# Paced mixer steps, later loads, turned units beside products and a re-ordered seam in a one-core hybrid mixer and ConvFFN kernel

## The chip, the cores and the metric

The kernel runs on one core of a Trainium2 chip. Its time is the device time of one execution in microseconds (us). Before the change it is 1338.61 us, the median of three runs (1338.36 to 1342.25).

## The reference

One step of a streaming encoder layer is computed for 1024 prompt tokens of a new stream and 32 tokens of a running one (D = 1024, FFN width 2816). Every matrix product is exact to fp32.

```python
xn = rms_norm(x, g)
parts = xn @ w_in                       # q, k, v, gates of three mixers
o = [gla(6 heads), hgrn2(5 heads), mlstm(5 heads)]   # linear recurrences with decay,
                                        # q/k of mlstm through a causal conv of width 4
h = head_rms_norm(concat(o), g_head) * silu(gate)
x = x + rms_norm(h @ w_out, g)          # sandwich norm
u, v = conv3(rms_norm(x, g) @ w_up)     # causal depthwise conv of width 3
y = x + rms_norm((gelu(u) * v) @ w_dn, g)
```

The outputs are the new x of both streams and all recurrent states.

## The kernel before

**Arithmetic.** A fp32 operand is held as two halves, h and l, in a reduced fp32 type. `mm3` (L86 to L90) makes one product of three matmuls: h by h (L88), l of one by h of the other (L89, L90). TensorE (PE) does all products and transposes (an `ident` operand); ScalarE (ACT) casts the h halves, VectorE (DVE) subtracts to get the l halves.

**Stages.** The 1024 prompt tokens are eight units of 128 tokens (0 to 7), the 32 sample tokens are unit 8. First comes `inproj`, which projects three groups g of units (0 to 2, 3 to 5, and 6, 7, 8). Before a group is projected its units are transposed on PE (tiles `xt30`, `xt31` are the two halves of unit 3), cast into `xh` by ACT and subtracted into `xl` by DVE. `pv<unit>_<block>` are products for values and gates, `pf2_0` to `pf2_13` are feature products (queries, keys, gates) of group 2, and `pv2_1_0` and the like are value products of group 2 in the other orientation, made after the features.

**Mixers beside products.** The recurrences of unit u (`mixer`) are generators that yield 12 times. `merge(main, nmain, nside)` steps a main generator and pumps mixer steps so that they advance in proportion. The mixers of group g-1 run beside the projection of group g; for group 2 there are 38 main steps and 36 mixer steps. In a mixer, `sc<u>_0`, `sc<u>_2` and `sc<u>_4` are three score products in short sub-blocks, each of which DVE masks into `P` (COPY_PREDICATED, L816) before the next may use the space; `mi` is one shared PSUM tile for transposes and state products (ACT copies it to `kt2`, L877); `og`, `oh`, `om`, `oi` are outputs, `hrs`/`hss` the head norms on POOL, `cat` the joined output (DVE L1002, POOL L1004). At its end the mixer of unit u stores `cat` to DRAM on SP's queue (`cat_d`) and the output projection loads it back as `ct`.

**Output projection.** `pipeline` runs `outproj` for units 0, 1, 2, 3, 8, 4, 5 (`RING`), each in steps: transposes `ctp<u>0`, `ctp<u>1` with their halves `ch`, `cl` (L1090, L1091), products `zp<u>0`, `zp<u>1`, norm and residual, and transposes `fxt<u>0`, `fxt<u>1` for the next stage. The mixers of units 6 and 7 run beside it. Units 6 and 7 are projected after the pipeline, in an order that is written out.

**Seam.** There the up projection of the FFN begins, a Strassen-like scheme with seven products and column operands B21, B11, T1, B22, T2, T4, T3, whose h half is cast on ACT (L1249) and whose l half is subtracted on DVE (L1250). The scheme runs block by block over the 1024 tokens in columns of 512; in the first one the operands come in two halves of 256, and the early halves of T2 and T4 lie in tiles with the names B22 and T1. So `B22l<-xg0` after 659 us is T2's l half and `T1l<-xg0` after it is T4's. `A12_1h`, `A11_1h` are weights of the next block; the two halves of a weight share a name in the trace and are told apart by engine (L93 on ACT casts, L94 on DVE subtracts). L1165 and L1166 scale unit 7's projection by its norm and add the residual.

**Order.** A scheduler lays the instructions of every engine out ahead of time; each engine then executes its row strictly in that order. Priorities, `issue_after` and the order of the generators' steps decide it.

**End.** `down_all` ends with four token tiles: L1873 adds the last partial product, L1711 squares, L1718 adds two partial sums on POOL, L206 and L207 make the reciprocal root, L1732 scales, and the result is stored.

## Time and profile before

| | us |
|---|---|
| median of three runs | 1338.61 |
| profiled execution | 1338.15 |
| its span | 1336.4 |
| PE busy | 1295.7 (97%) |
| DVE busy | 1009.2 (76%) |
| ACT busy | 700.0 (52%) |
| POOL busy | 284.6 (21%) |
| mean granted TensorE clock | 0.990 |

The profiled execution is 1338.15 us long, 1.75 us more than its span, and 0.46 us under the median. A busy PE is counted per matmul; in a row of the timeline the bracket at its end is the idle time of the engine just before it and what ended that. A windows row holds the stretch, its length, the busy time and instructions of PE, PE's weight loads, DVE, ACT and POOL, then the granted clock, the busy share of the DMA engines and GB/s.

### The profile page before, as it was taken

How to read it: one execution, taken by the hardware profiler on the slowest of the kernel's cores; microseconds unless marked ns; L12 is line 12 of the kernel's file. 1: busy time of each engine (PE TensorE's matmuls, PEld its weight loads, DVE VectorE, ACT ScalarE, POOL GpSimd, SP SyncE). 2: the span in 40 equal slices, each digit the busy share in tenths (PEclk: the TensorE clock that was granted, in tenths of full speed). 3: DMA queues.
4: the chain of work that ended last, by engine and by line, in shares of the span. 5: the costliest groups of instructions: out<-in, count | busy, mean ns of one | idle time of the engine just before them, and what ended most of it. 6: DMA issues, size and time to landing. Idle time of an engine off the chain costs nothing.

```text
span 1336.4 us, 25589 instructions
## 1 busy us (share of the span) xinstructions
PE 1295.7 (97%) x9896; PEld 1097.9 (82%) x9896; DVE 1009.2 (76%) x1761; ACT 700.0 (52%) x1298; POOL 284.6 (21%) x400
## 2 busy tenths in 40 slices
PE   6999999998999999999999999999999999999997
PEld 6999899998898987867887777778888887778885
DVE  5795659768588778785898776778888976499556
ACT  5655556554575555444764444444555454454552
POOL 4532302135022163223110010111110000020005
PEclk9999999999998999989999999999999999999999
DMA  9799878886789954534436988864665349844425
GB/s 336 246 360 367 280 258 260 275 278 214 260 263 309 330 180 163 184 111 135 143 133 216 365 223 284 213 185 135 158 162 145 88 147 350 330 146 148 139 87 126
DMA packets 134785, 291.73 MB, mean 218 GB/s; under 512 B 29016, under 2 KB 63992, under 8 KB 132536
## 3 DMA queue, kind: packets, MB, share of 16 engines
q1 hardware_dynamic: 120887, 266.51, 58.4%
q0 software_dynamic: 9264, 19.14, 7.8%
q10 hardware_dynamic: 4512, 4.46, 1.0%
q8 instruction: 77, 1.26, 0.4%
q14 instruction: 45, 0.36, 0.1%
HBM read 229.38 MB, written 85.78 MB: 236 GB/s over the span
## 4 chain that ended last, share of the span: by engine, by line
PE 63%; DVE 9%; ACT 2%; issue 1%; POOL 1%; DMA 0%; DVEq 0%; POOLq 0%; ACTq 0%
PE pux_None L88 4%; PE pux_None L90 4%; PE pux_None L89 4%; PE puw_None L89 3%; PE puw_None L90 3%; PE puw_None L88 3%; PE q L88 3%; PE q L89 3%; PE q L90 3%; PE x L88 2%; PE x L89 2%; PE x L90 2%; PE zp L88 2%; PE zp L90 2%; PE zp L89 2%; PE us L1475 2%
## 5 line engine op out<-in xcount | busy, mean ns | idle before, releaser
L1442 DVE SCALAR_TENSOR_TENSOR y<-uu,fconv_sb,y 128x1024 f32<-128x1024 f32 x88 | 112.8, 1281 | 24.7 <-ACT y L1440 23.7
L1439 POOL COPY fhalo<-uu 128x2 f32<-128x2 f32 x44 | 19.3, 439 | 380.7 <-DVE uu L1352 380.7
L1440 ACT ACTIVATE y<-uu,fconv_sb 128x1024 f32<-128x1024 f32 x44 | 54.7, 1244 | 12.8 <-DVE uu L1352 12.2
L88 PE MATMUL pv<-wt_0h,xh 128*128 128x256 f32 (+1 forms) x192 | 56.0, 292 | 2.8 <-DVE xl L319 1.6
L90 PE MATMUL zp<-woh,cl 128*128 128x512 f32 (+1 forms) x144 | 57.0, 396 | 1.5 <-DVE cl L1091 1.5
L88 PE MATMUL zp<-woh,ch 128*128 128x512 f32 (+1 forms) x144 | 56.5, 401 | 0.7 <-ACT ch L1090 0.7
L89 PE MATMUL zp<-wol,ch 128*128 128x512 f32 (+1 forms) x144 | 56.9, 395 | 0.0
L90 PE MATMUL pv<-wt_1h,xl 128*128 128x256 f32 (+1 forms) x192 | 55.1, 287 | 0.0
L90 PE MATMUL pv<-wt_0h,xl 128*128 128x256 f32 (+1 forms) x192 | 54.8, 286 | 0.0
L88 PE MATMUL pv<-wt_1h,xh 128*128 128x256 f32 (+1 forms) x192 | 54.8, 285 | 0.0
L89 PE MATMUL pv<-wt_0l,xh 128*128 128x256 f32 (+1 forms) x192 | 54.7, 285 | 0.0
L89 PE MATMUL pv<-wt_1l,xh 128*128 128x256 f32 (+1 forms) x192 | 54.5, 284 | 0.0
L206 POOL TENSOR_SCALAR hrs<-hss 128x5 f32<-128x5 f32 (+3 forms) x27 | 10.1, 375 | 174.2 <-DVE hss L1000 170.3
L1718 POOL TENSOR_TENSOR gss<-gss 128x1 f32<-128x1 f32 (+1 forms) x9 | 9.8, 1092 | 174.2 <-ACT gjk L1711 174.2
L816 DVE COPY_PREDICATED P<-masks_sb,sc 128x352 f32<-128x352 int32 (+3 forms) x53 | 37.8, 713 | 6.0 <-PE sc L729 5.4
L88 PEld LDWEIGHTS pv<-wt_0h,xh 128*128 128x128 f32 x192 | 36.2, 188 | 4.3 <-DVE xl L319 1.9
L88 PEld LDWEIGHTS pv<-wt_1h,xh 128*128 128x128 f32 x192 | 36.2, 189 | 0.7 <-issue 0.6
L1000 DVE TENSOR_REDUCE hss<-sq 128x5 f32<-128x320 f32 (+3 forms) x27 | 13.5, 502 | 30.7 <-ACT sq L999 30.6
L207 POOL TENSOR_TENSOR hrs<-hrs,mhalf 128x5 f32<-128x5 f32 (+3 forms) x27 | 36.2, 1341 | 2.2
L90 PEld LDWEIGHTS pv<-wt_0h,xl 128*128 128x128 f32 x192 | 36.4, 189 | 0.2
L89 PEld LDWEIGHTS pv<-wt_0l,xh 128*128 128x128 f32 x192 | 36.3, 189 | 0.1
L89 PEld LDWEIGHTS pv<-wt_1l,xh 128*128 128x128 f32 x192 | 36.2, 189 | 0.1
(1899 smaller groups left out, 4639.9 us busy)
## 6 DMA issues: line engine op xcount, KB each, us to landing
wus<-in_w_us SPq DMA_DIRECT2D x16, 1024.0 KB
wrP<-in_w_dn SPq DMA_DIRECT2D x27, 512.0 KB, 3.7
ht<-h_d SPq DMA_DIRECT2D x22, 512.0 KB, 7.9
wt_0r<-in_w_tok SPq DMA_DIRECT2D x21, 512.0 KB, 6.0
wt_1r<-in_w_tok SPq DMA_DIRECT2D x21, 512.0 KB, 6.1
h_d<-y SPq DMA_DIRECT2D x21, 512.0 KB, 4.4
ws_d<-in_w_dn POOLq DMA_DIRECT2D x20, 512.0 KB, 7.0
wrP<-ws_d SPq DMA_DIRECT2D x20, 512.0 KB, 3.9
```

The costliest lines, as they stand in the source:

```text
L88: pe.matmul(ps, lh[0], rh[0], start=first, stop=False, **kw)
L89: pe.matmul(ps, lh[0], rh[1], start=False, stop=False, **kw)
L90: return pe.matmul(ps, lh[1], rh[0], start=False, stop=last, **kw)
L206: pool.tensor_scalar(out, ss, 1.0 / width, eps, op0=ALU.mult, op1=ALU.add)
L207: pool.tensor_tensor(out, out, mhalf[:n, :cols], op=ALU.pow)
L816: dve.copy_predicated(dst, mk.broadcast_to([n, 11, *mk.shape[2:]]), src)
L1000: dve.tensor_reduce(ss[:n, h0:h0 + nh], sq3, axis=mybir.AxisListType.X, op=ALU.add)
L1439: behind["POOL"] = pool.tensor_copy(fhalo[:, j, :], u[:, SEQ - 2:SEQ])
L1440: act.activation(y, u, AF.Identity, scale=fconv[:, j, 2:3], bias=fconv[:, j, 3:4])
L1442: dve.scalar_tensor_tensor(y, uu[i][:, s:s + SEQ], fconv[:, j, s:s + 1], y, op0=ALU.mult, op1=ALU.add)
L1475: kept["us"] = pe.matmul(ps[DEC * q:DEC * q + DEC], smp_x[:, k, :], ring[i % 3][:, q, :], start=k == 0, stop=k == 7)
L1718: pool.tensor_tensor(ss[:n, 0:1], ss[:n, 2:3], ss[:n, 3:4], op=ALU.add)
```

## The change

1. **Turned units.** The three groups share one pair of tiles `xh_all`, `xl_all`. `inproj` receives the generator that turns the next group's units and steps it inside block 7, after unit 0's product. So units 3 and 6 are transposed between products of the group before, and the others follow one place earlier.
2. **Pace.** `merge` takes a table of (main step, mixer steps done) for group 2: one mixer step per main step in the first three, nine in the next seven, three in the seven after those, then one per step.
3. **Loads.** A mixer loads `v` one step later and `vm`, `gt` two steps later than before, all on SP's queue. The `cat_d` store goes from SP's queue to POOL's.
4. **Output projection.** Unit 6 yields like the others and is stepped inside the pipeline; unit 4's `fxt` uses another PSUM pool.
5. **Norms.** Square is taken with scale 1/32, so that two partial sums are means already and one POOL instruction adds both and eps; the separate POOL add (L1161, L1718) is gone.
6. **Seam.** T2's halves are made ahead of unit 6's last steps; unit 7's scaling (L1165) waits until T2's l half is done, unit 6's second square until T2's h half is.
7. **End.** The last add of `down_all` (L1873) gets a high priority.

```diff
-    def inproj(g, xh, xl, normed, scaled=None):
+    def inproj(g, xh, xl, normed, following, scaled=None):
...
                 vg_store(blk, u, off, n, ps)
+                if blk == 7 and not i:
+                    next(following)
                 yield
...
+    PACE = ((0, 0), (3, 3), (10, 12), (17, 15), (NIN, 3 * NMIX))
+    normed = [norm_group(g, *norm_tiles(g)) for g in range(3)] + [None]
...
-        merge(inproj(g, *xs_, norm_group(g, *xs_), scaled), NIN, n_side)
+        merge(inproj(g, *xs_, *normed[g:g + 2], scaled), NIN, n_side, PACE if g == 2 else None)
...
-            sp.dma_start(cat_d[t0:t0 + n, :], cat[:n])
+            pool.dma_start(cat_d[t0:t0 + n, :], cat[:n])
...
-            if u in RING:
+            if u != 7:
                 yield
-        if u not in RING:
+        if u == 7:
             yield
...
-        pool.tensor_tensor(ss[:n, 2:3], ss[:n, 0:1], ss[:n, 1:2], op=ALU.add)
-        rstd_of(ss[:n, 3:4], ss[:n, 2:3], n, 1, 1024)
+        rstd_of_halves(ss[:n, 3:4], ss[:n, 0:1], ss[:n, 1:2], n)
         if u == 7:
             for hf in range(2):
-                dve.scalar_tensor_tensor(pss[hf], pss[hf], ss[:, 3:4], gm[:, cs[hf]], op0=ALU.mult, op1=ALU.mult)
+                with tc.issue_after(kept["T2l"].ins):
+                    dve.scalar_tensor_tensor(pss[hf], pss[hf], ss[:, 3:4], gm[:, cs[hf]], op0=ALU.mult, op1=ALU.mult)
...
-    merge(pipeline(firsts), 26, 3 * NMIX + 2)
+    merge(pipeline(firsts, last[0]), 26, 3 * NMIX + 2)
...
     with tc.high_priority(offset=10 * AHEAD):
+        col_operands(px, q0, 0, res=X, parts="2", at_=early)
         next(last[0])
         with tc.issue_after(kept["t4"].ins):
             next(last[1])
-        col_operands(px, q0, 0, res=X, parts="t", at_=early)
+        col_operands(px, q0, 0, res=X, parts="4", at_=early)
...
-            dve.tensor_tensor(CA[:, i, 1], CA[:, i, 1], W[i], op=ALU.add)
+            with tc.high_priority(offset=AHEAD):
+                dve.tensor_tensor(CA[:, i, 1], CA[:, i, 1], W[i], op=ALU.add)
```

Three places show how the rows of the engines move. (Numbers behind the last underscore of a name only count the tiles.)

**PE, in the output projection, between the mixer of unit 7's second and third score product.** Before:

```order
L729 MATMUL sm7_8113<-ident_123,mqk7_7906 128x64
L88 MATMUL zp81_8323<-woh7_6898,ch81_8034 32x512
L89 MATMUL zp81_8323<-wol7_6906,ch81_8034 32x512
L90 MATMUL zp81_8323<-woh7_6898,cl81_8035 32x512
L1086 MATMUL ctp41_8386<-ident_123,ct4_7889 128x128 x4
L1195 MATMUL fxt30_8395<-ident_123,z3_7845 128x128 x4
L729 MATMUL sc7_4_8179<-Qz1_153,Ld1_151 64x2x32
```

The same place after the change, without the 20 matmuls in the middle of `zp40`:

```order
L738 MATMUL sm7_8105<-ident_123,mqk7_7899 128x64
L1207 MATMUL fxt30_8387<-ident_123,z3_7838 128x128 x4
L1207 MATMUL fxt31_8393<-ident_123,z3_7838 128x128 x4
L88 MATMUL zp40_8429<-woh0_6887,ch40_8246 128x512
L89 MATMUL zp40_8429<-wol0_6895,ch40_8246 128x512
...
L89 MATMUL zp40_8429<-wol7_6902,ch41_8383 128x512
L90 MATMUL zp40_8429<-woh7_6894,cl41_8384 128x512
L1097 MATMUL ctp50_8458<-ident_123,ct5_8239 128x128 x4
L738 MATMUL sc7_4_8171<-Qz1_153,Ld1_151 64x2x32
```

All 24 matmuls of `zp40`, and with them `fxt31` and `ctp50`, now stand ahead of `sc7_4`; `zp81` and `ctp41` have moved ahead of `sc7_2`.

**PE, in the features of group 2, where the transposes of unit 4's key wait for their PSUM tile.** Before, the second pair stands inside `pf2_12`:

```order
L88 MATMUL pf2_12_5572<-xh2_4320,wf2_12h_5568 128x288
L89 MATMUL pf2_12_5572<-xl2_4321,wf2_12h_5568 128x288
L90 MATMUL pf2_12_5572<-xh2_4320,wf2_12l_5569 128x288
L88 MATMUL pf2_12_5572<-xh2_4320,wf2_12h_5568 128x288
L89 MATMUL pf2_12_5572<-xl2_4321,wf2_12h_5568 128x288
L729 MATMUL mi_159<-ident_123,kh4_5305 128x128 x2
```

After the change it stands right behind `rows2` (the gates' rows, turned to columns) and ahead of `pf2_11`:

```order
L90 MATMUL pf2_10_5380<-xh_all_162,wf2_10l_5377 128x288
L629 MATMUL rows2_5433<-r_dc_2_5010,cf_sb_112 128x5 x3
L631 MATMUL rows2_5433<-ident_123,r_st_2_4999 128x128 x2
L631 MATMUL rows2_5433<-ident_123,r_st_2_4999 32x128
L738 MATMUL mi_159<-ident_123,kh4_5161 128x128 x2
L88 MATMUL pf2_11_5451<-xh_all_162,wf2_11h_5447 128x288
```

The pair has moved ahead of 29 products; `sc4_0` and the first pair have moved ahead too, in front of `pf2_10`.

**DVE, in the seam, around the l half of the weight A12 of the second block.** Before:

```order
L1352 TENSOR_TENSOR uu0_8877<-c6_00_8991,puw0_0_8913 128x256
L1250 TENSOR_TENSOR B22l_8834<-xg1_8868,B22h_8833 128x4x128
L1425 TENSOR_TENSOR uu0_8877<-uu0_8877,puv0_0_8940 128x256
L1199 TENSOR_TENSOR xg1_8868<-fxt71_9034,gcols_sb_108 128x4x128
L94 TENSOR_TENSOR A12_1h_9106<-wu1r_8972,A12_1h_9106 128x512
```

After the change:

```order
L1271 TENSOR_TENSOR xg2_8947<-xg1_8857,xg2_8947 128x4x128
L1363 TENSOR_TENSOR uu1_8867<-c5_00_8963,pux0_0_8899 128x256
L1363 TENSOR_TENSOR uu1_8867<-c7_00_9072,puz0_0_8901 128x256
L1275 TENSOR_TENSOR xg1_8857<-xg1_8857 128x1024
L1262 TENSOR_TENSOR B22l_8823<-xg1_8857,B22h_8822 128x4x128
L94 TENSOR_TENSOR A12_1h_9093<-wu1r_8959,A12_1h_9093 128x512
```

The two additions into `uu1` and the large subtraction (L1263 before, L1275 now) stood behind A12's l half and now stand ahead of it; the two additions into `uu0` have moved further up.

## The prediction

> **What bounds the kernel now.** I first cut the span into its stages and compared busy time with length (the windows view: start and end, length, then busy time and instructions of PE, its weight loads, DVE, ACT, POOL, then the granted clock).

> ```profile
> 130.00:350.00 220.00, 214.40 (x2582) 199.62 (x2581) 156.40 (x362) 124.81 (x256) 67.59 (x94) 0.99 0.79 259
> 350.00:690.00 340.00, 324.74 (x3586) 278.94 (x3586) 270.13 (x587) 190.90 (x409) 90.18 (x143) 0.97 0.60 195
> 690.00:1326.00 636.00, 636.00 (x2916) 503.03 (x2915) 484.81 (x666) 313.84 (x511) 73.08 (x100) 1.00 0.63 196
> 1326.00:1336.40 10.40, 0.76 (x4) 0.29 (x2) 6.04 (x9) 0.72 (x2) 3.21 (x7) 0.68 0.40 151
> ```

> From 690 to 1326 us PE is busy all the time at full clock. The change removes no matmul, so nothing is to be had there. PE stands idle for 220 - 214.40 = 5.6 us in the first stretch and 15.3 us in the second, and in both the clock is below 1. The last 10 us hold no products; a chain over DVE, ACT and POOL ends the kernel there. What the change can give lies in these idle times, the half-speed stretches and the last chain. Next I looked for the single waits in PE's timeline (the bracket is the wait ahead of the row and what ended it):

> ```profile
> 141.72 0.39 PE L88 MATMUL pv<-wt_0h,xh 128*128 128x256 f32 x1 [0.83 <-DVE vth L425]
> ...
> 322.44 0.81 PE L729 MATMUL oi<-C,mqz 128*64 128x65 f32 x20 [0.90 <-DVE cat L1002]
> ...
> 325.43 0.66 PE L315 MATMUL xt<-ident,x 128*128 128x128 f32 x4 [0.72 <-ACT vth L98]
> ...
> 329.45 0.45 PE L88 MATMUL pv<-wt_0h,xh 128*128 128x282 f32 x1 [1.64 <-DVE xl L319]
> ...
> 384.28 0.80 PE L729 MATMUL oi<-C,mqz 128*64 128x65 f32 x20 [0.84 <-DVE cat L1002]
> ...
> 398.82 0.44 PE L729 MATMUL mi<-ident,kh 128*128 128x128 f32 x2 [0.38 <-ACT kt L877]
> ...
> 401.66 0.67 PE L729 MATMUL sc<-Qz,k 64*64 64x64 f32 x32 [0.68 <-DVE P L816]
> ...
> 413.18 1.14 PE L729 MATMUL sc<-Qz,Ld 64*64 64x64 f32 x64 [2.15 <-DVE e L543]
> ...
> 588.87 1.80 PE L729 MATMUL sc<-Qz,Ld 64*64 64x64 f32 x64 [2.44 <-DVE P L816]
> ...
> 626.93 1.26 PE L1086 MATMUL ctp<-ident,ct 128*128 128x128 f32 x8 [0.42 <-DVE z L1199]
> ...
> 628.93 0.50 PE L88 MATMUL zp<-woh,ch 128*128 128x512 f32 x1 [0.75 <-ACT ch L1090]
> ...
> 631.12 0.50 PE L90 MATMUL zp<-woh,cl 128*128 128x512 f32 x1 [1.46 <-DVE cl L1091]
> ...
> 660.80 0.39 PE L89 MATMUL pux<-B22l,S_0h 128*128 128x256 f32 x1 [0.67 <-DVE B22l L1250]
> ```

> Then the granted clock behind the three longest of them, and around those of 0.42, 0.75 and 1.46 us:

> ```profile
> 329.60:333.10 3.50, 3.50 (x16) 3.49 (x17) 3.50 (x14) 1.76 (x5) 1.96 (x2) 0.51 0.67 267
> ...
> 415.00:422.00 7.00, 7.00 (x63) 6.39 (x63) 5.91 (x13) 1.43 (x4) 0.00 (x0) 0.51 0.73 204
> ...
> 589.00:596.00 7.00, 7.00 (x121) 6.33 (x120) 6.56 (x12) 1.15 (x2) 0.54 (x2) 0.51 0.24 80
> ...
> 625.00:650.00 25.00, 22.38 (x110) 17.96 (x109) 18.73 (x24) 16.66 (x36) 3.41 (x8) 1.00 0.44 147
> ```

> Behind the waits of 1.64, 2.15 and 2.44 us PE ran at half speed for 3.5, 7 and 7 us, which loses 0.49 of each: 1.7, 3.4 and 3.4 us. The group with 1.46 us (631.12) left the clock full, as the last row shows. I therefore price a wait of 1.6 us or more with such a stretch behind it, where PE was also short of work around it.

> [...]

> **The change part by part**, against the profiled time of 1338.15 us (0.46 under the median).

> *Third score product of unit 7.* Before, PE has little to do between the second and the third score product:

> ```profile
> 584.47 0.27 PE L729 MATMUL sm<-ident,mqk 64*128 64x64 f32 x1
> ...
> 587.80 0.92 DVE L816 COPY_PREDICATED P<-masks_sb,sc 128x352 f32<-128x352 int32 x1
> ...
> 595.96 0.48 PE L88 MATMUL zp<-woh,ch 128*128 128x512 f32 x1
> ...
> 601.30 0.39 PE L90 MATMUL zp<-woh,cl 128*128 128x512 f32 x1
> ```

> The mask copy ends at 588.72, 4.0 us behind `sm`. In the new order `zp40` stands between (24 matmuls from 595.96 to about 601.5, so 5.5 us at full clock), and two transposes beside it (1.2 us). Cover 6.7 us against 4.0 needed: the wait of 2.44 goes, and the 3.4 us of half speed with it. **-5.8** (bounds -2.4, if the clock falls there anyway, and -5.8).

> *Unit 6's projection.* `ctp60` moves ahead of `zp51`, `ctp61` between the `fxt4` halves; casts and subtractions then lie beside 24 products. The waits of 0.42, 0.75 and 1.46 go: **-2.6** (bounds -1.5 and -2.6).

> *Seam.* T2's l half needs only its ACT cast, and DVE makes it before unit 7's scaling instead of after: the wait of 0.67 goes. But the third product of the pair now follows in the same PSUM tile and must wait for ACT's copy (first row), +0.4, and A12's l half falls behind three operations that stood after it:

> ```profile
> 658.97 0.35 ACT L1347 COPY c<-pux 128x256 f32<-128x256 f32 x1
> ...
> 670.83 0.68 DVE L94 TENSOR_TENSOR A_1h<-wu1r,A_1h 128x512 fp32r<-128x512 f32 x1
> ...
> 671.98 0.40 PE L90 MATMUL puy_None<-B21h,A_1h 128*128 128x512 f32 x1
> ...
> 672.63 1.22 DVE L1263 TENSOR_TENSOR xg<-xg 128x1024 f32<-128x1024 f32 x1
> ...
> 674.37 0.41 DVE L1352 TENSOR_TENSOR uu<-c,pux 128x256 f32<-128x256 f32 x1
> ```

> 1.22 + 2 x 0.41 = 2.0 later than 671.5, of which I take off 0.5 for waits of DVE in that stretch. PE used A12's half 0.5 us after it was there, so it waits about 1.4, less two small waits near it. In sum **+1.0** (bounds -0.9, if the three fit in DVE's own waits, and +2.4).

> *End.* The last add stood behind a scaling that has nothing to do with it, and one POOL add lay in the chain:

> ```profile
> 1328.05 0.75 DVE L1732 SCALAR_TENSOR_TENSOR fr<-ca,gss,fr 128x512 f32<-128x512 f32 x1
> ...
> 1328.71 0.68 DVE L1873 TENSOR_TENSOR ca<-ca,q 128x512 f32<-128x512 f32 x1
> ...
> 1330.28 0.70 POOL L1718 TENSOR_TENSOR gss<-gss 128x1 f32<-128x1 f32 x1 [2.35 <-ACT gjk L1711]
> ...
> 1331.07 0.19 POOL L206 TENSOR_SCALAR gss<-gss 128x1 f32<-128x1 f32 x1
> ```

> Moved ahead of the second scaling of that tile and of its own queue's delay, the add gains 0.8. Of POOL's first two steps one goes; the first after a rest takes 0.70, the second 0.19 and 0.08 to start, so I take 0.3. **-1.1** (bounds -0.3 and -1.7). The same add goes from the tiles of the output projection too; PE waits for none of those, so nothing.

> *Turned units 3, 4 and 5.* `xt30`, `mi` and `xt31` now stand ahead of `pv1_7`, whose 24 matmuls covered ACT's work. The second pair of `mi` has to wait for ACT to empty the first:

> ```profile
> 143.00 0.39 ACT L98 ACTIVATE vth<-pv 128x256 f32<-128x256 f32 x1
> ...
> 145.40 0.73 ACT L877 COPY kt<-mi 64x256 f32<-64x256 f32 x2
> ...
> 150.53 0.58 ACT L318 CAST xh<-xt 128x512 fp32r<-128x512 f32 x1
> ```

> Behind 143.0 ACT runs 0.39, 0.58 and 0.73, so to 144.7; PE starts `xt30` at 141.7 as it now starts `pv`, needs about 0.7 for it (the rate of the `xt` row above) and 0.1 for one `mi`, and waits 2.2. A second wait of 0.4 for `xl`, less 0.3 that is saved, makes 2.3 less small overlaps: +2.0. It is longer than 1.64, in a place with few other products, so I add that stretch's 1.7. **+3.7** (bounds +0.5 and +3.7).

> *Turned units 6, 7 and 8.* The products of block 7 stand between `xt60` and the `xl` that was waited for; of the old 0.90, 0.72 and 1.64 us about as much stays in smaller pieces, since DVE is behind there: oi 1.9 instead of 0.9, the others 0.5, 0.5 and 1.1. That is +0.7, with the half-speed stretch of 1.7 gone: **-1.0** (bounds -3.4 and +1.7).

> *Pace and loads in group 2.* The steps of unit 3 and 4 come earlier against the products, so the 0.84 and 0.68 go. The third score product of unit 4 stands ahead of `pv2_1_0` now, but behind `pf2_12` and `pf2_13` undivided; the mask copy is the end of a DVE row that has no gaps there, and I find it 2.4 us earlier and PE's wait 1.8 instead of 2.15, with the same half-speed stretch. The new price is at the second pair of `mi`:

> ```profile
> 394.36 0.38 PE L88 MATMUL pf<-xh,wf_11h 128*128 128x288 f32 x1
> ...
> 397.62 0.29 PE L88 MATMUL pf<-xh,wf_12h 128*128 128x288 f32 x1
> ...
> 398.02 0.74 ACT L877 COPY kt<-mi 64x256 f32<-64x256 f32 x2
> ```

> Before, PE came there at 398.44. Without `pf2_11` (3.26), five of `pf2_12` (0.6) and the 0.84 it comes at 393.7. ACT's copy stands behind its casts and gates as before and I find it ending at 396.5, so PE waits 2.8 instead of 0.38. Sum -0.84 - 0.68 - 0.35 + 2.4 = **+0.5** (bounds -7, if both waits and the clock's loss go, and +4, if the copy stays at 398.8 and the clock falls once more).

> The later loads and the store on POOL's queue: the loads' first users come a step later still, and PE waited for a `cat_d` load once. POOL's small copies of the convolution's edge now stand behind the store; their reader has several us to spare. Nothing, but see the second rival.

> Sum: -5.8 - 2.6 + 1.0 - 1.1 + 3.7 - 1.0 + 0.5 = -5.3, so 1332.8 against the profile and **1333.3** against the median.

> **The rivals.**

> *The clock falls at every new wait* (0.24). Three waits of about 2 us are new or stay (322, 394, seam). If each brings 1.7 more, the sum is -0.2: 1338.4. For it: three of three waits above 1.6 us did so. Against: 660 to 680 us is full of large products.

> *POOL's queue becomes a wait* (0.11, the slower side). The store of `cat` must wait for its last scaling; the convolution's edge copies, the gates `vg` and the next norms of that queue stand behind it. Where it is issued later than those copies' readers need them, ACT's row stops with them, and DVE and PE next. It decides once the store comes over about 4 us later than its neighbours. At 2.44 us, the longest wait seen, for six units: +14.6, so 1348.

> *The mixers run so far ahead that group 2 has no wait at all* (0.17). Then group 2 gives -7 and units 3 to 5 only +0.5: -16, so 1322.6. For it: DVE and ACT have idle time before 390 us, which the earlier steps use.

> *The clock has nothing to do with the waits* (0.06). Then -2.4, -2.6, +1.0, -1.1, +2.0, +0.7, +0.5: -1.9, so 1336.7. Against it stand the three rows of the clock. [...]

> *The forecast* has 0.42.

> **How the numbers follow.** A measurement of this kernel can tell about 0.3%, that is 4 us, so faster ends at 1334.6. Of the forecast's own 0.42 some 0.31 lies below that (its bounds reach further down than up), 0.09 within and 0.02 above; the third rival is faster; 0.04 of the first and 0.01 of the last come out faster. The first rival's rest is the same but for 0.03, the last's rest is the same, the second is slower. Faster 0.53, same 0.31, slower 0.16. The range reaches to the third rival below and above the first: 1323.5 to 1342.

> **What would show it.** Right: no wait ahead of `sc7_4` and full clock there; no wait at `ch`, `cl` of unit 6; the last add 0.8 us sooner behind the last matmul; new waits at `mi` behind `xt30` and `rows2`, and at A12. Wrong: half speed still in 580 to 600 us, or no new wait at `mi`. PE idle between 690 us and the end would overturn the whole.

## The result and the profile after

The changed kernel takes **1327.89 us** (median of four, 1325.50 to 1330.28), the kernel before beside it 1339.73 us. The ratio is 0.991, with a 95% interval from 0.9884 to 0.9935: 0.9% faster, within the range given. The gain is 11.8 us, more than twice the 5.3 us of the forecast's sum. The profiled execution has 1326.90 us with a span of 1325.1 us, 11.3 us less than before.

The windows view of the changed kernel, with the columns of the prediction's first fence (the third row ends with the last product):

```profile
130.00:350.00 220.00, 214.54 (x2598) 200.20 (x2597) 154.14 (x362) 126.99 (x262) 68.69 (x99) 0.99 0.78 259
350.00:690.00 340.00, 330.16 (x3618) 283.96 (x3617) 280.99 (x603) 195.83 (x415) 94.59 (x139) 0.98 0.63 208
690.00:1316.00 626.00, 626.00 (x2871) 494.58 (x2869) 475.92 (x653) 306.28 (x501) 68.60 (x92) 1.00 0.64 191
1316.00:1325.00 9.00, 0.05 (x1) 0.00 (x0) 5.23 (x9) 0.72 (x2) 3.37 (x4) 0.71 0.47 175
```

From 690 us on nothing changed but the start: PE is busy throughout, as before. In the second stretch PE's idle time fell from 15.3 to 9.8 us, and its clock rose from 0.97 to 0.98. PE's timeline shows the waits that are left (what was L729 is L738 now, L88 to L90 are the same):

```profile
144.21 0.44 PE L738 MATMUL mi<-ident,kh 128*128 128x128 f32 x2 [2.07 <-ACT kt L888]
...
323.91 0.30 PE L738 MATMUL oi<-C,mqz 128*64 128x65 f32 x3 [1.07 <-DVE cat L1013]
...
394.34 0.44 PE L738 MATMUL mi<-ident,kh 128*128 128x128 f32 x2 [3.10 <-ACT kt L888]
395.09 0.58 PE L88 MATMUL pf<-xh_all,wf_11h 128*128 128x288 f32 x1 [0.31 <-DVE q L567]
...
588.88 1.14 PE L738 MATMUL sc<-Qz,Ld 64*64 64x64 f32 x64 [0.19 <-DVE P L827]
...
658.47 0.50 PE L88 MATMUL puy_None<-B21h,A_1h 128*128 128x512 f32 x1 [1.55 <-ACT A_1h L93]
659.51 0.50 PE L88 MATMUL pux_None<-B11h,A_1h 128*128 128x512 f32 x1 [0.31 <-ACT A_1h L93]
660.59 0.52 PE L90 MATMUL puy_None<-B21h,A_1h 128*128 128x512 f32 x1 [0.35 <-DVE A_1h L94]
```

The three new waits stand where the prediction had them: at `mi` behind `xt30` (2.07), at `mi` behind `rows2` (3.10), and at A12 (1.55). The wait of 2.44 us ahead of unit 7's third score product is 0.19 us now; those at `ctp`, `ch` and `cl` of unit 6 are gone. The clock around these places:

```profile
145.60:149.00 3.40, 3.40 (x24) 2.95 (x23) 3.08 (x9) 1.89 (x5) 2.04 (x4) 0.51 0.56 154
394.80:398.20 3.40, 3.11 (x13) 3.14 (x14) 3.34 (x9) 3.34 (x11) 0.58 (x2) 0.51 0.94 295
589.00:596.00 7.00, 7.00 (x135) 5.80 (x137) 4.76 (x9) 0.32 (x1) 0.00 (x0) 1.00 0.35 98
661.00:664.40 3.40, 3.40 (x10) 2.63 (x9) 3.40 (x6) 0.00 (x0) 0.00 (x0) 0.51 0.00 0
```

Half speed follows the new waits, and 589 to 596 us runs at full clock. At the end:

```profile
1315.66 0.39 PE L90 MATMUL q<-P3w,P3h 128*128 128x512 f32 x1
...
1317.21 0.68 DVE L1884 TENSOR_TENSOR ca<-ca,q 128x512 f32<-128x512 f32 x1
...
1318.81 1.18 POOL L211 TENSOR_SCALAR gss<-gss 128x1 f32<-128x1 f32 x1 [1.09 <-ACT gjk L1722]
```

The last add starts 1.16 us behind the last product's end (1316.05); before, it was 1.95 us (1328.71 less 1326.76). POOL's one instruction takes 1.18 us here, more than the two of before together (0.70, 0.08 to start, 0.19), so its part of the gain did not come.

To see where the time went, I cut the profiled executions at the first product of a few tiles: from `pv0_0` to `pf1_0` (units 3 to 5 are turned in it), to `pf2_2` (units 6 to 8), to `zp20` (group 2 and the start of the output projection), to `zp50` (the mixer of unit 7), to `zp70` (unit 6's projection), to `puy4` (the seam). Behind it lie 587.9 us in both.

| us | to pf1_0 | to pf2_2 | to zp20 | to zp50 | to zp70 | to puy4 | end |
|---|---|---|---|---|---|---|---|
| before | 186.4 | 171.7 | 161.8 | 83.1 | 28.5 | 95.9 | 9.6 |
| after | 188.7 | 167.2 | 160.1 | 77.9 | 25.0 | 97.8 | 9.1 |
| difference | +2.3 | -4.5 | -1.7 | -5.2 | -3.5 | +1.9 | -0.5 |
| predicted | +3.7 | -1.0 | +0.5 | -5.8 | -2.6 | +1.0 | -1.1 |

Over the stretches up to `puy4`, PE's idle time fell by 5.8 us (21.44 to 15.69) and the time at half speed from 20.5 to 17.1 us, which is worth 1.7. The other 3.2 of 10.7 us are busy time. It is the same 7205 matmuls, in fewer pieces (PE goes over to another output tile 358 times instead of 388); that this is the reason is not shown.

### The profile page after: what moved, and what is told of

Read it like the earlier page. It is cut to its first block, busy times and chain, and to the rows that moved or that the text cites. A ratio compares the mean times of both kernels' runs of the same rounds, so it can differ in the third digit from the quotient of the medians.

```text
span 1325.1 us, 25585 instructions
## 1 busy us (share of the span) xinstructions
PE 1290.7 (97%) x9896; PEld 1095.0 (83%) x9896; DVE 1008.1 (76%) x1761; ACT 700.0 (53%) x1298; POOL 286.1 (22%) x390
## 3 DMA queue, kind: packets, MB, share of 16 engines
q8 instruction: 77, 1.26, 0.4%
## 4 chain that ended last, share of the span: by engine, by line
PE 73%; DVE 14%; DMA 4%; ACT 4%; issue 3%; POOL 2%; SPq 0%; DVEq 0%; POOLq 0%; ACTq 0%
PE pux_None L88 4%; PE pux_None L90 4%; PE pux_None L89 4%; PE puw_None L90 3%; PE puw_None L88 3%; PE puw_None L89 3%; PE q L88 3%; PE q L90 3%; PE q L89 3%; PE pv L88 3%; PE pv L89 2%; PE pv L90 2%; PE x L88 2%; PE x L89 2%; PE x L90 2%
## 5 line engine op out<-in xcount | busy, mean ns | idle before, releaser
L88 PE MATMUL pv<-wt_0h,xh_all 128*128 128x256 f32 (+1 forms) x192 | 56.1, 292 | 0.9 <-DVE xl_all L326 0.7
L89 PE MATMUL zp<-wol,ch 128*128 128x512 f32 (+1 forms) x144 | 57.0, 396 | 0.0
L88 PE MATMUL zp<-woh,ch 128*128 128x512 f32 (+1 forms) x144 | 57.0, 405 | 0.0
L90 PE MATMUL zp<-woh,cl 128*128 128x512 f32 (+1 forms) x144 | 56.6, 394 | 0.0
L90 PE MATMUL pv<-wt_0h,xl_all 128*128 128x256 f32 (+1 forms) x192 | 54.7, 285 | 0.0
L89 PE MATMUL pv<-wt_0l,xh_all 128*128 128x256 f32 (+1 forms) x192 | 54.6, 284 | 0.0
L88 PE MATMUL pv<-wt_1h,xh_all 128*128 128x256 f32 (+1 forms) x192 | 54.3, 283 | 0.0
L89 PE MATMUL pv<-wt_1l,xh_all 128*128 128x256 f32 (+1 forms) x192 | 54.3, 283 | 0.0
L90 PE MATMUL pv<-wt_1h,xl_all 128*128 128x256 f32 (+1 forms) x192 | 54.3, 283 | 0.0
L206 POOL TENSOR_SCALAR hrs<-hss 128x5 f32<-128x5 f32 (+3 forms) x27 | 10.7, 396 | 171.1 <-DVE hss L1011 166.5
L88 PEld LDWEIGHTS pv<-wt_0h,xh_all 128*128 128x128 f32 x192 | 36.4, 190 | 2.2 <-DVE xl_all L326 1.1
L89 PEld LDWEIGHTS pv<-wt_0l,xh_all 128*128 128x128 f32 x192 | 36.4, 190 | 0.1
L90 PEld LDWEIGHTS pv<-wt_0h,xl_all 128*128 128x128 f32 x192 | 36.4, 189 | 0.1
L88 PEld LDWEIGHTS pv<-wt_1h,xh_all 128*128 128x128 f32 x192 | 36.0, 187 | 0.3 <-issue 0.2
L89 PEld LDWEIGHTS pv<-wt_1l,xh_all 128*128 128x128 f32 x192 | 35.9, 187 | 0.1
```

The source lines that it names most:

```text
L88: pe.matmul(ps, lh[0], rh[0], start=first, stop=False, **kw)
L89: pe.matmul(ps, lh[0], rh[1], start=False, stop=False, **kw)
L90: return pe.matmul(ps, lh[1], rh[0], start=False, stop=last, **kw)
L206: pool.tensor_scalar(out, ss, 1.0 / width, eps, op0=ALU.mult, op1=ALU.add)
```

## The experiments

What stood to be tested: do the terms belong to the edits to which I put them down, and does the length of a wait decide the clock? All experiments but one start from the changed kernel. Times are medians; a profiled execution lies up to 4 us beside its median.

**Turning of units.** Only unit 6 turned beside products, and no unit at all:

```diff
-                if blk == 7 and not i:
+                if blk == 7 and not i and g == 1:
                     next(following)
```

> Only unit 6 is turned beside the products of the group before; unit 3 is turned where it was before the change. Numbers against the changed kernel's profiled 1326.90 us. Theory (the turned units cost 2.2 us at units 3 to 5, by a wait of 2.07 us at the second pair of mi and the half-speed stretch behind it, and bring 4.5 us at units 6 to 8): that wait and the half speed at 145 to 149 us go, 1324.7. Rival 1 (both placings belong together, since an earlier unit 3 lets all mixers behind it start earlier): units 6 to 8 and group 2 lose as much as units 3 to 5 win, 1326.9 or above. Rival 2 (the half-speed stretch does not belong to the wait): 1324.8 to 1325.3, with a half-speed stretch still near 145 to 200 us.

```diff
-                if blk == 7 and not i:
-                    next(following)
```

> No unit is turned beside products; all else as changed. Numbers against the changed kernel's profiled 1326.90 us. Theory: 2.2 us come back at units 3 to 5 and 4.5 us are lost at units 6 to 8, with the waits of 0.90, 0.72 and 1.64 us at oi, xt and pv there as before and a half-speed stretch of 3.4 us behind the last: 1329.2. Rival (the prediction's own terms, 3.7 us cost and 1.0 us gain): 1324.2. Rival 2 (the gain at units 6 to 8 came from the paced steps and the later loads and not from the turned unit): units 6 to 8 stay short, 1324.7.

Without any turning the kernel takes 1328.78 us (ratio to before 0.9917, 0.9891 to 0.9942), 0.9 more than the changed kernel, which the intervals can't tell apart. Its stretch to `pf1_0` is 187.7 us and that to `pf2_2` 173.4, against 188.7 and 167.2 with both turned, so the signs are right: the placing costs in the first and brings more in the second. 1.7 of the 173.4 come from half speed at 355.5 to 358.8 us, and 1.7 of the 187.7 from half speed at 174.5 to 177.9 us, though no long wait stands ahead of the first: from 352.0 to 355.4 us PE was busy for 3.40 of 3.40 us, almost only with small products (matmuls of 64 or fewer columns, or on 16 rows); the last section comes back to that. The profiled execution is 3.8 us above its median, so its trace overstates the difference; the theory's 1329.2 fits the median.

With unit 6 alone it takes **1336.33 us** (0.9973, 0.9958 to 0.9988), 8.4 us more. Only rival 1 allows for that, and not for its reason. The wait at `mi` in units 3 to 5 is gone (1.0 us less in that stretch), and the stretch to `pf2_2` takes 2.0 us more; but the stretch from `zp20` to `zp50`, almost 400 us behind the edit (unit 3 is turned at 141 us), takes 85.1 us instead of 77.9. PE's timeline there:

```profile
550.16 0.92 PE L738 MATMUL og<-v,P 64*64 64x64 f32 x24 [1.21 <-DVE P L827]
...
571.11 0.44 PE L738 MATMUL mi<-ident,kh 128*128 128x128 f32 x2 [0.90 <-ACT kt L888]
...
573.18 0.41 PE L88 MATMUL zp<-woh,ch 128*32 128x512 f32 x1 [1.63 <-DVE z L1211]
```

None of these waits is in the changed kernel. The scheduler (called the planner from here on) has laid PE's row out differently: all three score products of unit 7 stand ahead of `ctp41` and `zp40`. I call this the third order; the first is that of before, the second that of the changed kernel (both are in the rows of PE shown with the change). Nothing in the program's text of that stage differs.

**The pace.** The table left out, then the loads and the store too:

```diff
-        merge(inproj(g, *xs_, *normed[g:g + 2], scaled), NIN, n_side, PACE if g == 2 else None)
+        merge(inproj(g, *xs_, *normed[g:g + 2], scaled), NIN, n_side, None)
```

> The pace table is left out; the mixers of group 1 advance evenly beside group 2 again, all else as changed. Numbers against the changed kernel's profiled 1326.90 us. Theory (the pace is worth about 3.3 us: it replaces waits of 0.84 and 0.68 us and the wait of 2.15 us at the third score product of unit 4, with 6.8 us of half speed, by one of 3.10 us at mi with 3.4 us): 1330.2, with a wait near 2.2 us at sc4_4 and a half-speed stretch of 6.8 us behind it, and no long wait at mi. Rival 1 (the prediction's term: the pace costs 0.5 us): 1326.4. Rival 2 (the later loads and the turned units brought it, not the table): 1326.9 with the wait at sc4_4 gone all the same.

It takes **1339.64 us** (ratio to before 1.0002, 0.9986 to 1.0017): without the table the whole gain of 11.8 us is gone, where the theory gave the table 3.3. PE's timeline in group 2:

```profile
411.46 0.35 PE L738 MATMUL sc<-Qz,Ld 64*64 64x64 f32 x9 [4.04 <-DVE e L552]
...
454.15 0.48 PE L738 MATMUL mi<-ident,mqk 128*128 128x128 f32 x1 [2.46 <-ACT kt L888]
```

The first is the old wait at unit 4's third score product, 4.04 instead of 2.15 us: the mask copy, one operation ahead of the one that the row names, ends at 411.3 us in DVE's full row. That is 1.7 us sooner than in the kernel before, while PE comes there 3.6 us sooner (407.4 instead of 411.0): 14 products of `pv`, which lay in between, are done by then. Counted from the first product of `pf2_2` DVE's copy is no sooner at all (43.4 us behind it, 43.5 before); with the pace it ends 41.0 us behind it. So an earlier PE is worth nothing here until DVE's work is put earlier too. The stretch to `zp20` takes 170.8 us instead of 160.1 (in an execution 2.9 us above its median), and that to `zp50` 83.7: the third order once more.

```diff
+        v = mx.tile([128, 704], F32, tag="v", name=f"v{u}", bufs=1)
+        sp.dma_start(v[:n], v_d[t0:t0 + n, :704])
+        vmt = vm[0]
+        sp.dma_start(vmt[:n, :, :64], v_d[t0:t0 + n, 704:].rearrange("t (h d) -> t h d", d=64))
+        gt = mx.tile([128, 1024], F32, tag="gt", name=f"gt{u}", bufs=1)
+        sp.dma_start(gt[:n], g_d[t0:t0 + n, :])
...
-        v = mx.tile([128, 704], F32, tag="v", name=f"v{u}", bufs=1)
-        sp.dma_start(v[:n], v_d[t0:t0 + n, :704])
...
-            pool.dma_start(cat_d[t0:t0 + n, :], cat[:n])
+            sp.dma_start(cat_d[t0:t0 + n, :], cat[:n])
```

> The changed kernel without the pace table and with v, vm, gt loaded where they were and the store of cat on its old queue. Numbers against the changed kernel's profiled 1326.90 us; without the table alone it was 10.0 us at the start of the output projection (9.3 behind, 0.7 of it from before group 2) and 7 to 8 us in it. Theory (with even steps the later loads and POOL's store cost, so taking them back brings group 2 to what it was before the change, about 4.5 us behind the changed kernel; the order of the output projection is the third one again, 5.8 us): 1337.2. Rival (the loads and the store do nothing): as without the table, 1339.6 or more, the wait of 4.0 us at sc4_4 and that of 2.5 us at mi as there.

It takes 1337.30 us (0.998, 0.9969 to 0.9991), as the theory had it (1337.2). The stretch to `zp20` is 164.5 us: the wait of 4.0 us stays, that of 2.46 us is gone (ahead of it ACT had stood 2.39 us for a store of `vg`). Between these two executions the later loads and the store cost 6.3 us there; the medians of twelve runs each lie only 2.3 us apart, so how much they cost with even steps stays open.

The same edit of the loads with the pace kept:

> The changed kernel with v, vm, gt loaded where they were and the store of cat on its old queue, the pace table kept. The order of the output projection stays that of the changed kernel. Numbers against the changed kernel's profiled 1326.90 us. Theory (the pace carries the gain in group 2, the loads are worth nothing beside it): within 1 us of 1326.9. Rival 1 (the prediction's second rival turned round: the store on POOL's queue costs, so taking it back gains): 1325 or less. Rival 2 (the earlier loads hold SP's queue or the buffers back, so that a mixer step waits for them): 1330 or more, with new waits on a load in DVE's or ACT's row.

It takes 1327.43 us (0.9905, 0.9888 to 0.9923): no difference from the changed kernel. Beside the pace the loads and the store together are worth nothing. So the 14.6 us of the prediction's slower rival, the store on POOL's queue, did not come; the store was not put back by itself.

**Unit 6 in the pipeline**, undone:

```diff
-            if u != 7:
+            if u in RING:
...
-    merge(pipeline(firsts, last[0]), 26, 3 * NMIX + 2)
+    merge(pipeline(firsts), 26, 3 * NMIX + 2)
```

> Unit 6's projection is not stepped inside the pipeline (the output-projection part of the change undone), all else as changed. Numbers against the changed kernel's profiled 1326.90 us. Theory: the wait of 2.44 us ahead of the third score product of unit 7, the half-speed stretch behind it (5.0 us together) and the waits at ctp60, ch and cl (3.5 us) come back: 1335.4. Rival 1 (the clock has nothing to do with the wait): 2.4 and 2.6 us come back, 1331.9, and the clock around 589 us is full. Rival 2 (the paced steps and the loads brought the gain at sc7_4 and not the new order of the output projection): only the 3.5 us come back, 1330.4.

It takes 1331.28 us (0.9935, 0.9915 to 0.9955), 3.4 more: rival 2. The stretch to `zp50` stays at 78.0 us without a wait at unit 7, and that to `zp70` takes 30.1:

```profile
621.25 1.25 PE L1097 MATMUL ctp<-ident,ct 128*128 128x128 f32 x8 [0.42 <-DVE z L1211]
623.26 0.50 PE L88 MATMUL zp<-woh,ch 128*128 128x512 f32 x1 [0.75 <-ACT ch L1101]
625.45 0.50 PE L90 MATMUL zp<-woh,cl 128*128 128x512 f32 x1 [1.45 <-DVE cl L1102]
```

These are the three waits of before, to 0.01 us. So this part brings unit 6's own term and nothing of the 5 us at unit 7.

**The norms.** Which edit had moved unit 7's score product? The one that I had priced at nothing: POOL's add in the tiles of the output projection. It alone put back:

```diff
-        rstd_of_halves(ss[:n, 3:4], ss[:n, 0:1], ss[:n, 1:2], n)
+        pool.tensor_tensor(ss[:n, 2:3], ss[:n, 0:1], ss[:n, 1:2], op=ALU.add)
+        rstd_of(ss[:n, 3:4], ss[:n, 2:3], n, 1, 1)
         if u == 7:
```

> The output projection alone has its separate POOL add of the two partial sums back (nine tiles, one small instruction each, at the place it had before); all else as changed. In the planner's order this puts the third score product of unit 7 ahead of unit 4's product again. Numbers against the changed kernel's profiled 1326.90 us. Theory (the gain at that score product comes from the order alone, and the order was turned by POOL's shorter chain): the wait of about 2.4 us and half speed near 585 us come back, 5.0 us, 1331.9. Rival 1 (the prediction: the add in these tiles is worth nothing, and unit 6 stepped inside the pipeline brought the gain): 1326.9. Rival 2 (the clock has nothing to do with the wait): 1329.3.

It takes 1332.06 us (0.9951, 0.9932 to 0.9969), 4.2 more; the theory had 1331.9. PE's row is in the first order again, and the wait is back in its old place:

```profile
585.87 0.34 PE L738 MATMUL sc<-Qz,Ld 64*64 64x64 f32 x8 [2.45 <-DVE P L827]
```

And the kernel before with this edit alone:

```diff
-            act.activation(z[:n, cs[hf]], ps[:n], AF.Square, accum_out=ss[:n, hf:hf + 1])
+            act.activation(z[:n, cs[hf]], ps[:n], AF.Square, scale=1.0 / 32, accum_out=ss[:n, hf:hf + 1])
...
-        pool.tensor_tensor(ss[:n, 2:3], ss[:n, 0:1], ss[:n, 1:2], op=ALU.add)
-        rstd_of(ss[:n, 3:4], ss[:n, 2:3], n, 1, 1024)
+        pool.tensor_scalar(ss[:n, 3:4], ss[:n, 0:1], ss[:n, 1:2], EPS, op0=ALU.add, op1=ALU.add)
+        pool.tensor_tensor(ss[:n, 3:4], ss[:n, 3:4], mhalf[:n, :1], op=ALU.pow)
```

> The kernel before, with nothing changed but the norms of the output projection (the square with scale 1/32, one POOL instruction fewer in each of nine tiles). The planner's order of the output projection becomes a third one: the three score products of unit 7 stand earlier than in either kernel, zp40 behind all of them. Numbers against the kernel before's profiled 1338.15 us; the stretch from the first product of zp20 to the first of zp50 took 83.1 us there, 77.9 us in the changed kernel, and 83.7 us in the run without the pace, which has this third order. Theory (only the order that the planner comes to counts, and edits do not add up): 83.7 us, 1338.8, with waits at og of unit 7 and at zp80, zp81 and none of 2.4 us at the third score product. Rival 1 (the norm edit by itself carries the gain of 5 us there, since putting it back cost that): 78 us, 1333.0. Rival 2 (it does nothing without the other edits): 83.1 us, 1338.2, the wait of 2.4 us in its old place.

It takes 1337.74 us (0.9992, 0.9977 to 1.0007): no change, with the waits of the third order.

```profile
555.27 0.92 PE L729 MATMUL og<-v,P 64*64 64x64 f32 x24 [1.37 <-DVE P L816]
...
576.15 0.44 PE L729 MATMUL mi<-ident,kh 128*128 128x128 f32 x2 [0.90 <-ACT kt L877]
...
578.22 0.42 PE L88 MATMUL zp<-woh,ch 128*32 128x512 f32 x1 [1.63 <-DVE z L1199]
```

The stretch takes 82.1 us (1.6 under the 83.7 expected, since here the clock stayed full behind the last wait, 1.00 from 577 to 595 us). So the same edit brings 3.7 us in one program (81.6 to 77.9) and about 1 us in another (83.1 to 82.1, the clock's luck included).

**The seam**, undone:

```diff
-                with tc.issue_after(kept["T2l"].ins):
+                if True:
...
-        with tc.issue_after(kept["T2"].ins) if u == 6 else ExitStack():
+        if True:
...
-        col_operands(px, q0, 0, res=X, parts="2", at_=early)
...
-        col_operands(px, q0, 0, res=X, parts="4", at_=early)
+        col_operands(px, q0, 0, res=X, parts="t", at_=early)
```

> The seam part is undone (T2 and T4 made together behind the last units' steps, unit 7's scaling and unit 6's second square wait for nothing more); all else as changed. Numbers against the changed kernel's profiled 1326.90 us. Theory (the seam part costs 1.9 us, by the waits of 1.55, 0.31 and 0.35 us for the halves of A12 and the half speed behind them, less the 0.67 us for T2): 1325.0, full clock at 661 to 665 us. Rival 1 (the prediction's term of 1.0): 1325.9. Rival 2 (the waits at A12 come from DVE's work as a whole and stay, T2's wait comes back as well): 1327.6.

It takes 1328.40 us (0.9915, 0.9898 to 0.9932), not to be told from the changed kernel; the theory's 1325.0 is missed, rival 2 fits. The wait at T2 is 0.72 us again, and PE waits 1.22 us for A12's l half:

```profile
652.17 0.39 PE L89 MATMUL pux<-B22l,S_0h 128*128 128x256 f32 x1 [0.72 <-DVE B22l L1262]
...
664.30 0.68 PE L90 MATMUL puy_None<-B21h,A_1h 128*128 128x512 f32 x1 [1.22 <-DVE A_1h L94]
```

The stretch to `puy4` takes 97.5 us against 97.8, both with a half-speed step (1.7). With the new seam but full clock it takes 96.4 us in five other runs; with the old seam and full clock 95.9 (before) and 96.2 (norms alone). The seam part itself costs about 0.4 us. The wait of 1.22 us is not that of the kernel before (0.24 us for A11's h half there), but it is in the run of the norms alone, too: it came with the norms.

Those copies that stand ahead of A12's cast on ACT, moved to POOL:

```diff
-                        act.copy(t[:, :, :256], e)
+                        pool.tensor_copy(t[:, :, :256], e)
```

> The changed kernel, with the four copies of the early halves of T2 and T4 into the whole tiles made by POOL, which is idle in the seam, and not by ACT, where they stand 4.2 us ahead of the cast of A12's first half. Numbers against the changed kernel's profiled 1326.90 us. Theory (the waits of 1.55, 0.31 and 0.35 us at A12 are due to those copies): 2.2 us less, and 1.7 us more where half speed followed, 1323.0 to 1324.7. Rival 1 (DVE's own row is as late there): 1326.5, a wait of similar size for A12's l half. Rival 2 (POOL's copies are slow and the whole T2 and T4 come late): 1328 or more, with a new wait at the products with T2 or T4 of the second block.

It takes 1331.67 us (0.9944, 0.9927 to 0.9961), 3.8 more. A12 no longer waits, but others do:

```profile
655.87 1.09 PE L1207 MATMUL fxt<-ident,z 128*128 128x128 f32 x8 [1.51 <-ACT z L1190]
...
657.98 0.39 PE L88 MATMUL puy<-B21h,A_0h 128*128 128x256 f32 x1 [1.02 <-ACT B21h L1261]
...
659.24 0.56 PE L89 MATMUL puy<-B21l,A_0h 128*128 128x256 f32 x1 [0.87 <-DVE B21l L1262]
```

Freed of the copies, ACT's row was laid out anew, and PE's transposes and early products with it; they now come before their operands. The time is rival 2's, the place is not.

**The two waits at `mi`.** The second pair of transposes in another PSUM tile, for units 0 and 4:

```diff
-                kps = small(2, 128)
+                kps = psm.tile([128, 2, 128], F32, tag="o", name=f"kp{u}", bufs=2) if f0 and u in (0, 4) else small(2, 128)
```

> The changed kernel, with the second pair of key transposes of units 0 and 4 in a PSUM tile of the outputs' pool instead of the shared tile mi, so that PE need not wait for ACT to empty the first pair. Numbers against the changed kernel's profiled 1326.90 us. Theory (the waits of 2.07 and 3.10 us at mi with 3.4 us of half speed behind each are pure loss): 8.5 us less, 1318.4, full clock at 145 and 395 us. Rival 1 (DVE and ACT are behind there, and the next score products wait instead): 1 to 3 us less, 1325, with new waits at sc of unit 0 or 4. Rival 2 (the clock has nothing to do with the waits): 5.2 us less, 1321.7, with two more half-speed stretches elsewhere.

It takes 1328.82 us (0.9918, 0.9906 to 0.9930): no gain. The place is rival 1's; of its 1 to 3 us nothing came.

```profile
144.63 0.56 PE L738 MATMUL sc<-Qz,k 64*64 64x64 f32 x25 [2.51 <-issue]
...
398.02 0.61 PE L88 MATMUL pf<-xh_all,wf_11h 128*128 128x288 f32 x1 [4.34 <-DVE q L567]
```

The next instruction waits instead, and longer: the score product, and `pf2_11` for its PSUM bank. In the changed kernel `pf2_11` already waited 0.31 us for the same DVE operation, right behind the wait of 3.10: that small row said beforehand that the long one had a second wait behind it.

**The clock.** Eleven waits of different length, in the down projection:

```diff
...
+                if (kind, p) in LADDER:
+                    for j in range(2):
+                        with tc.issue_after(behind["PE"].ins):
+                            behind["PE"] = pe.matmul(banks[3][:16], zero, w[0], start=False, stop=False,
+                                                     skip_group_check=True)
+                        for _ in range(0 if j else LADDER[kind, p]):
+                            pool.memset(zero.bitcast(F32), 0.0)
```

> The changed kernel with eleven waits made on purpose in the down projection, where PE was busy all the time at full clock: two small products with zeros (they add nothing to the sums), and between them 3 to 18 small POOL instructions for which the second one waits, so waits from about 0.5 to 3.5 us, each on its own. It measures what kind of wait lowers the clock. Theory 1 (the clock is set anew in steps of 3.41 us, and a step is at half speed where PE was idle for 1.6 us or more of the step before): no stretch behind waits below 1.5 us, one behind each above 3.2 us, and of those between only where most of the wait lies in one step. Theory 2 (the prediction's: the length of the wait decides, from 1.6 us up): a stretch behind every wait of 1.6 us or more. Theory 3 (only an idle step of 3.4 us does it): none, or one behind the longest alone. The whole takes about 1360 us.

It took 1373.43 us in its one execution (the last wait became 11.8 us, since POOL had other work there). Four of the waits in PE's timeline:

```profile
1186.42 0.41 PE L1711 MATMUL q<-P4w,zero 128*16 128x512 f32 x1 [2.48 <-POOL zero L1714]
...
1233.37 0.55 PE L1711 MATMUL x<-P6w,zero 128*16 128x512 f32 x1 [2.14 <-POOL zero L1714]
...
1257.83 0.61 PE L1711 MATMUL q<-P5w,zero 128*16 128x512 f32 x1 [3.15 <-POOL zero L1714]
...
1272.72 0.41 PE L1711 MATMUL q<-P5w,zero 128*16 128x512 f32 x1 [1.97 <-POOL zero L1714]
```

And the clock (the last column but two) behind each of them, in the same order:

```profile
1186.50:1189.90 3.40, 3.40 (x16) 2.79 (x17) 3.40 (x7) 2.15 (x6) 1.08 (x1) 1.00 0.14 58
...
1233.50:1236.90 3.40, 3.40 (x9) 2.62 (x9) 0.69 (x1) 0.62 (x1) 0.00 (x0) 0.50 0.00 0
1257.40:1260.80 3.40, 2.97 (x8) 2.30 (x9) 0.69 (x1) 0.62 (x1) 0.26 (x3) 0.50 0.00 0
1272.80:1276.20 3.40, 3.40 (x16) 2.79 (x17) 0.69 (x1) 0.91 (x2) 0.00 (x0) 1.00 0.00 1
```

The wait of 2.48 us left the clock full, that of 2.14 did not. That excludes a limit on the length of the wait, theory 2. Two half-speed stretches of this run start seven times 3.413 us apart (1257.364 - 1233.471 = 7 x 3.413); the last section has the starts in the kernels before and after, which lie on such a grid too. Laid on it, the wait of 2.14 us lies in one step; that of 2.48 is cut into 1.74 and 0.74. A step ran at half speed where PE had been idle for 2.14 or 2.68 us of the step before, and at full speed after 1.47, 1.63, 1.64, 1.71, 1.74 and (behind a wait of 2.06 us that nobody made, at 1100.6) 1.85 us. Theory 1 fits these steps, with its limit between 1.85 and 2.14 us instead of 1.6; theory 3 falls with the 2.14.

No run beat the changed kernel; that without the later loads is its equal.

## Why the prediction was right or wrong

**The third score product** (-5.8, measured -5.2). The wait and the half speed behind it went because `zp40` covers the mask copy: right in place, mechanism and size. What failed is a passage at the end of another part: "The same add goes from the tiles of the output projection too; PE waits for none of those, so nothing." That PE does not wait for the add does not make it worth nothing: without it the planner lays PE's row out in another order, and that is where these 5 us come from. I had read the new order and never asked which edit made it. The runs show that the edit decides (its return alone brought the wait back) and that undoing unit 6's pipeline leaves the order alone. They show, too, that the edit does so only beside some of the others: alone, without the pace, or with unit 6 alone turned, the third order comes, while with no unit turned the second one stays (78.0 us to `zp50`, 0.20 us of waiting at the third score product). Why was not traced; that the transposes of the norm's result are ready earlier in the planner's reckoning is a guess.

**Unit 6's projection** (-2.6, measured -3.5): the three waits went as said; 0.9 us of PE's busy time went with them, which I had not counted.

**Group 2** (+0.5, measured -1.7). The new wait at `mi` was forecast at 2.8 us and is 3.10. The step that failed is "PE's wait 1.8 instead of 2.15" at the third score product of unit 4, "with the same half-speed stretch": neither is left there. The mask copy did come as much earlier as I had found: counted from the first product of `pf2_2` it ends at 41.0 us instead of 43.5, 2.5 sooner for 2.4. It is PE that comes 2.3 us later than the sum has it (at 41.6 for 39.3), 0.6 behind the copy's end. Half speed follows the wait at `mi` (0.51 from 394.8 to 398.2 us) and takes 1.7 us, which my own rule asked for and the sum left out; 0.3 more of that wait and 0.31 at `pf2_11` make up the rest. So PE pays once, at `mi`, and not a second time. One of the two waits of the third rival is gone, then, but not because the mixers ran further ahead. And the term hides what the pace is worth: against even steps it brings 10.7 us in this stretch of the profiled executions (170.8 to 160.1).

**Turned units 3 to 5** (+3.7, measured +2.3): the wait is 2.07 for 2.2, with its half-speed step. The second wait, of 0.4 for `xl`, did not come. But the 2.3 is a lucky execution: eight others with unit 3 turned this way have the same wait (2.04 to 2.08 us) and take 189.3 to 190.7 us for this stretch, 2.9 to 4.3 more than before, seven of them with two half-speed steps. The forecast's 3.7 lies in the midst of these.

**Turned units 6 to 8** (-1.0, measured -4.5). I left 4.0 us of waits there, "since DVE is behind"; 1.8 us were left (1.07, 0.51, 0.23). That is the step that failed, and not in this part alone: in the run with unit 6 alone turned `oi` waits 1.95 us, as I had priced it (1.9), and it is unit 3's earlier turn that brings it to 1.07. The clock's 1.7 went as said, and 1.3 us of busy time beyond that.

**The seam** (+1.0, measured +1.9): the wait of 0.67 at T2 went and the one for ACT's copy came (0.46 for 0.4), as said. The wait at A12 is 1.55 for 1.4, but it is not the wait that I had worked out. Mine was for the l half, on DVE. In the trace PE stops for the h half, which ACT casts behind its four copies (its end is 658.41, PE goes on at 658.47), and then 0.35 us for the l half:

```profile
657.79 0.62 ACT L93 CAST A_1h<-wu1r 128x512 fp32r<-128x512 f32 x1
```

```profile
659.85 0.68 DVE L94 TENSOR_TENSOR A_1h<-wu1r,A_1h 128x512 fp32r<-128x512 f32 x1
```

So the likeness of the two numbers is luck: the sum has nothing for ACT's row there. DVE's lateness is there as well: with the h half in time PE would wait about 2.2 us for the l half (1.55, 0.31 and 0.35 together, an estimate from these rows). In itself the part costs 0.4; the rest is a half-speed step that falls there in one execution and not in another. Of the changed kernel and of the run with POOL's add back:

```profile
657.50:660.80 3.30, 1.68 (x5) 0.81 (x6) 3.30 (x7) 3.26 (x7) 0.00 (x0) 1.00 0.00 0
661.00:664.40 3.40, 3.40 (x10) 2.63 (x9) 3.40 (x6) 0.00 (x0) 0.00 (x0) 0.51 0.00 0
```

```profile
660.20:663.60 3.40, 1.85 (x14) 1.50 (x13) 3.40 (x7) 3.40 (x7) 0.00 (x0) 1.00 0.33 5
663.70:667.00 3.30, 2.63 (x10) 1.72 (x10) 3.30 (x7) 1.75 (x4) 0.00 (x0) 1.00 0.00 0
```

Both have the same waits of 1.55, 0.31 and 0.35 us (the last is 0.36 in the second), and in both the grid cuts them in two. In the first, 1.60 us lie in one step and half speed follows; in the second, 1.55 us, and it does not. In the ten profiled executions with the wait of 1.55 us, half speed came behind 1.60, 1.63, 1.86, 1.86 and 1.94 us in one step, full speed behind 1.33, 1.33, 1.55, 1.55 and 1.55.

**The end** (-1.1, measured -0.5): the add's 0.8 is right, POOL's 0.3 was not to be had.

**The clock.** "A wait of 1.6 us or more" was the wrong rule, though it gave the right answer for every wait of the changed kernel but the one in the seam. That the 1.46 us of before "left the clock full" was chance: in the run without unit 6 in the pipeline the same 1.45 us are followed by half speed (0.50 from 626.2 to 629.6 us). The rival by which the clock has nothing to do with waits falls: the waits of 2.14 and 3.15 us made in the down projection were followed by 0.50, where the changed kernel has 1.00 from 690 to 1316 us.

In sum most of the waits that I named came and went as forecast. The two terms that were off the most, by 5.7 of the 6.0 us in all, are those in which PE was to wait for DVE; the smaller misses of the other terms cancel nearly.

## What to carry to other kernels

Where a planner lays out the rows, an edit's price is not that of its instructions alone: compare the rows of every engine with each edit put back singly, before putting a gain down to the edit that was meant to bring it. Here one small instruction in each of nine tiles, on an engine that is mostly idle, turned an order that is worth 4 us, and one edit almost 400 us ahead cost 8. When a wait is to be removed, look what its successor waits for; a small wait right behind a long one is the next one in line. And a row that is late on DVE is mended by putting DVE's work earlier, not by bringing PE there sooner.

## What the runs showed of the hardware

Where the steps fall against the program differs between executions: the waits at A12, the same to 0.01 us, had 1.60 us in one step in the changed kernel and 1.55 us in the run with POOL's add back, and half speed, a loss of 1.7 us, followed in the first alone. That can explain part of the 5 us between the changed kernel's four executions, but I have not split that up.

Idle time is not all that counts. In the changed kernel PE is busy for 3.24 of 3.40 us, mostly with small products of the 32 sample tokens, and half speed follows:

```profile
486.80:490.20 3.40, 3.24 (x64) 2.47 (x63) 3.31 (x13) 3.40 (x8) 2.13 (x4) 1.00 0.72 144
490.40:497.00 6.60, 6.60 (x48) 5.39 (x46) 6.41 (x12) 5.34 (x7) 1.42 (x3) 0.50 0.87 316
```

The kernel before has such a stretch, too, of 3.413 us from 496.9 us, behind 3.24 of 3.40 us busy (493.5 to 496.9 us). In the run with POOL's add back half speed (0.50 from 588.5 to 591.9 us) came behind a step with 0.79 us of idle time (585.1 to 588.5 us), and in the run without turning (0.50 from 355.5 to 358.8 us) behind one with none (3.40 of 3.40 us busy from 352.0 to 355.4 us, in 87 matmuls). What it is in these steps that half speed goes with was not shown: no run tried the small products by themselves.
